# Token order in a one-core encoder step: prefix, prompt, sample; queries without the prefix's rows; value keys in blocks of 128; the third phase's operand sums in one run

## The chip, the core and the metric

The kernel runs on one core of a Trainium2 chip. The core has a matrix engine (TensorE, PE in the profile, with its weight loads in a row of their own, PEld), a vector engine (DVE), a scalar/activation engine (ACT), GpSimd (POOL) and SyncE (SP), which issues nearly all DMAs here. Data lies in on-chip memory of 128 partitions; matmul results go to eight PSUM banks of 128 x 512 fp32. The metric is device time in microseconds for one launch, the median of several runs.

## The reference, cut to what matters

One layer of an encoder on two kinds of rows: a new stream of 512 prompt frames with 16 learned prefix rows ("meta tokens") in front, and 64 sample frames of a running stream that has 128 cached rows.

```python
xp = concat([meta, x_prompt])                 # 16 + 512 rows
h = rmsnorm(x);  z = h @ w_in                 # 2048 -> 1024 q | 1024 k | 1024 v | 512 cq | 256 ckv | 64 kr
# group A, 8 heads: two softmaxes with a shared relative-position bias, p = p0 - lam * p1, o = p @ v, rmsnorm
# group B, 8 heads: q = rmsnorm(cq) @ w_uq, latent keys and values from rmsnorm(ckv) @ w_ukv, one rotary key
# chunk-causal: a frame sees its own chunk of 64 frames, all earlier ones, and the prefix
x = x + concat([o_a, o_b]) @ w_out
h = rmsnorm(x);  x = x + (silu(h @ w_gate) * (h @ w_up)) @ w_down      # 2048 -> 5632 -> 2048
y_prompt = rmsnorm(xp)[16:];  y_sample = rmsnorm(xs)                  # the prefix's own output isn't returned
# also returned: keys, values, latents and rotary keys of prefix + prompt, and of the sample
```

So the prefix's rows are needed as keys and values only, never as queries.

## The kernel before, in words

All 592 rows (T) are columns: activations lie transposed, 128 features by rows. Matrix products are made of three matmuls in a reduced-precision fp32 format, each operand split in a high and a low part: ACT copies the high part (`split`, a copy on ACT), DVE subtracts it from the source for the low part. With two column halves, one 128 x 128 weight block costs six matmuls. The order of columns is sample (64), prefix (16), prompt (512); `OWN` = 80 is sample and prefix together, `TQ` = 576 the rows that are asked as queries, `QH` = 288 its half, `TH` = 296 the half of T.

Phase 1 reads the rows (`load_x`), transposes them on TensorE (`transpose_x`, six pieces of the token list `tok`), sums squares for the norm on ACT (`squares`), and then runs the 31 column blocks of `w_in` as projections of 16 x 6 matmuls (`project`). Group A's heads run between them: scores (`scores`), softmax, and `probabilities_times_values`, which transposes the probabilities on TensorE into one PSUM bank ("tp"), has ACT and DVE evict and split them, and multiplies. Its keys go in pieces: the 80 own columns, then four blocks of 128 prompt keys, then the sample's cached and own keys.

Phase 2 does group B the same way, with the output projection's first half (`mix_out`) as filling between the heads. In phases 1 and 2 the order of TensorE's instructions is written out: `Streams` runs generators against a planned clock (each matmul advances it, each bank is taken and given back at planned times), and TensorE keeps that program order. Other engines' instructions are ordered by a planner from their readiness, each engine then runs its own queue strictly in order.

Phase 3 is the output projection's second half: for each of 16 rows of blocks two halves of 24 matmuls, with weights fetched and split two halves ahead (`fetch`), the residual added, the row scaled (`xg`), its square accumulated on POOL (`sq2`, `rb2`), and for every second row the seven operands of a Strassen-Winograd product (`token_operands`), four of them sums made on POOL. Phase 4 is the feed-forward with those operands (`winograd`), then the final norm, transposes and output DMAs (`finish`), which go through the token halves of 288 in groups of 96 rows.

In `token_operands` POOL's sums share a tile, one overwriting the other after its operand was split:

```python
t = sum_tile()
pin(G.tensor_tensor(t, b12, b11, op=ALU.subtract))
operand(m, 5, t)
yield
pin(G.tensor_tensor(t, b22, t, op=ALU.subtract))
operand(m, 6, t)
```

and the phase's loop runs the whole generator at once:

```python
if i % 2:
    for _ in token_operands(ma, i // 2, xe, xg):
        pass
```

Of the kernel before, what the change touches and what calls it, by code (L numbers as in the profile page):

```python
# [19 lines left out]
P = 128  # L20
# [4 lines left out]
T = OWN + SEQ  # L25
TH = T // 2
TP = T + PAST
TQ = NS + SEQ
QH = TQ // 2
KEPT = ((0, NS, 0), (OWN, SEQ, NS))  # L30
# [101 lines left out]
def encoder_step(  # L132
# [78 lines left out]
    def project(ps, wsrc, xs, dup=False):  # L211
        for hf in range(2):
            wh, wl = weights(
                wsrc[hf * 8 * P:(hf + 1) * 8 * P, :].rearrange("(k p) c -> p k c", p=P), 8, P, dup)
            for k in range(8):
                kc = hf * 8 + k
                mm3([ps[:, 0, 0:TH], ps[:, 1, 0:TH]], wh[:, k, :], wl[:, k, :],
                    halves(xs[kc][0]), halves(xs[kc][1]), kc == 0, kc == KC - 1)
                yield 0

    def probabilities_times_values(pt_b, p5, vkeys, vpast, pool, tbank, pso, pace, done):
# [6 lines left out]
        def times_values(n, p, c0):  # L228
            (vh, vl), (ph, pl) = vkeys[n], p
            for m, (a, b) in enumerate(((vh, ph), (vh, pl), (vl, ph))):  # L230
                PE.matmul(po[:, c0:512], a, b, start=(n == 0 and m == 0), stop=(n == 4 and m == 2))
# [3 lines left out]
        yield from st.take("tp")  # L235
        tp = tbank()
        for b in range(4):
            PE.transpose(tp[0:OWN, b * P:(b + 1) * P], pt_b[b][:, 0:OWN], ident)
        hi, lo = evac("po", tp, OWN, 512)
        last = [(0, (hi[0:OWN], lo[0:OWN]), 0)]  # L240
        st.give("tp", 1.9)
        for t in range(2):
            yield pace
            yield from st.take("tp")
            w = 512 - P * t
            tp = tbank()
            for b in range(t, 4):
                PE.transpose(tp[:, (b - t) * P:(b - t + 1) * P], pt_b[b][:, OWN + t * P:OWN + (t + 1) * P], ident)
            hi, lo = evac(f"pk{t}", tp, P, w)
            for a in last:  # L250
                times_values(*a)
            last = [(1 + t, (hi, lo), t * P)]
            st.give("tp", 1.9)
        yield pace
        yield from st.take("tp")
        tp = tbank()
        for n, (t, b) in enumerate(((2, 2), (2, 3), (3, 3))):
            PE.transpose(tp[:, n * P:(n + 1) * P], pt_b[b][:, OWN + t * P:OWN + (t + 1) * P], ident)
        hi, lo = evac("pk2", tp, P, 384)
        for a in last:  # L260
            times_values(*a)
        last = [(3, (hi[:, 0:256], lo[:, 0:256]), 256), (4, (hi[:, 256:384], lo[:, 256:384]), 384)]
        st.give("tp", 1.7)
        yield pace
        yield from st.take("tp")
        tp = tbank()
        PE.transpose(tp[:, 0:NS], p5[:, 0:P], ident[0:NS, 0:NS])
        PE.transpose(tp[0:NS, NS:2 * NS], p5[:, P:P + NS], ident[0:NS, 0:NS])
        p5h = pool.tile([P, 2 * NS], F32R, name="p5h")
        p5l = pool.tile([P, 2 * NS], F32R, name="p5l")  # L270
        for rows, c in ((P, slice(0, NS)), (NS, slice(NS, 2 * NS))):
            split(p5h[0:rows, c], p5l[0:rows, c], tp[0:rows, c])
        for a in last:
            times_values(*a)
        done(po, NS, TQ)
        st.give("tp", 1.7)
# [5 lines left out]
        own = [v[0:NS] for v in vkeys[0]]  # L282
        for (vh, vl), ph, pl in ((vpast, p5h[:, 0:NS], p5l[:, 0:NS]),
                                 (own, p5h[0:NS, NS:2 * NS], p5l[0:NS, NS:2 * NS])):
# [3 lines left out]
        done(po5[:, 0:NS], 0, NS)  # L288
        st.give("po", 1.0)

    def scores(b, sp, passes):

        if b == 4:
            n, W, q0 = NS, P + NS, 0
            pieces = [(0, 0, P, T), (0, P, NS, 0)]
            flat = True
        else:
            n, W, q0 = P, 144 + P * b, OWN + P * b
            flat = W <= 512
            pieces = [(0, 0, W, NS)] if flat else [(0, 0, W // 2, NS), (1, 0, W // 2, NS + W // 2)]  # L300
        for bank, o, w, k0 in pieces:
            for i, (q, k) in enumerate(passes):
                PE.matmul(sp[0:n, bank, o:o + w], q[:, q0:q0 + n], k[:, k0:k0 + w],
# [11 lines left out]
    def sum_squares(pq, tiles, tile_of):  # L315
        for n, z in enumerate(tiles):
            sq = tile_of("sq")
            S.activation(sq, z, AF.Square)
            yield 1.2
            for i in range(2):  # L320
                PE.matmul(pq[:, i, 0:TH], ones, sq[:, i * TH:(i + 1) * TH],
# [19 lines left out]
    with ExitStack() as ph:  # L341
# [21 lines left out]
        xs1 = list(zip(xh, xl))  # L363
        rb = az.tile([P, T], F32, name="rb")
# [5 lines left out]
        tok = [(0, OWN), (OWN, P), (208, 88), (TH, P), (424, P), (552, 40)]  # L370
# [4 lines left out]
        with tc.tile_pool(name="xn", bufs=1) as xn, tc.tile_pool(name="xc", bufs=1, side="right") as xc:  # L375
# [11 lines left out]
            ssp = az.tile([P, 6, 4], F32, name="ssp")  # L387
# [4 lines left out]
            def load_x(cg):  # L392
                cs = slice(cg * 512, (cg + 1) * 512)
                for j, (o, n) in enumerate(tok):
                    t = xn.tile([P, 512], F32, name="xn", tag=f"xn{j}", bufs=4)
                    if j == 0:
                        load(t[0:NS, :], x_sample[:, cs])
                        load(t[NS:OWN, :], meta[:, cs])
                    else:
                        load(t[0:n, :], x_prompt[o - OWN:o - OWN + n, cs])  # L400
                    xt_in[cg, j] = t

            def transpose_x(kc):
                cg, k = kc // 4, kc % 4
                if kc % 2 == 0:
                    sp = sbig("pxt")
                    banks = [sp[:, 0, 0:TH], sp[:, 1, 0:TH]]
                else:
                    banks = [tbank("pxa")[:, 0:TH], pso.tile([P, 512], F32, name="pxb", tag="po")[:, 0:TH]]
                for j, (o, n) in enumerate(tok):  # L410
                    b = o // TH
                    PE.transpose(banks[b][:, o - b * TH:o - b * TH + n],
                                 xt_in[cg, j][0:n, k * P:(k + 1) * P], ident[0:n, 0:n])
                xt = xn.tile([P, T], F32, name="xt", tag="xt", bufs=7)
                g = gA[:, kc:kc + 1]
                if kc % 2 == 0:
                    split_scaled(hv(xh[kc]), hv(xl[kc]), ev(sp), g)
# [1274 lines left out]
```

## Time and profile before

| | |
|---|---|
| median of 3 runs | 2481.91 us (2481.8 to 2481.93) |
| the profiled execution: its time, its span | 2478.58 us, 2476.8 us |
| granted TensorE clock, mean | 0.994 |
| busy share of the span: PE, PEld, DVE, ACT, POOL | 97%, 95%, 72%, 47%, 30% |
| start up to the first full stretch of matmuls | 0 to about 25 us |
| phase 1 | to about 550 us |
| phase 2 | to 842.7 us |
| phase 3 | 842.7 to 960.1 us |
| phase 4 and output | 960.1 to 2476.8 us |

Busy time counts a matmul from its start to a modelled end, so neighbouring matmuls overlap; what one costs in a stream is the distance from start to start. In the timeline a line stands for a run of like instructions: start, busy time, engine, line, operation, output<-input, shape, count, and in brackets how long the engine sat idle before it and who released it. In the rows by line and form the idle time before a group stands behind the bar, with its releasers. In the waits: who waited for whom, total microseconds, times, the longest. Line 125 and lines 108 and 112 are helpers through which ACT, DVE and SP, and TensorE's ordered matmuls and transposes, are issued, so tiles tell more than lines there.

### The profile page before, as it was taken

How to read it: one execution, taken by the hardware profiler on the slowest of the kernel's cores; microseconds unless marked ns; L12 is line 12 of the kernel's file. 1: busy time of each engine (PE TensorE's matmuls, PEld its weight loads, DVE VectorE, ACT ScalarE, POOL GpSimd, SP SyncE). 2: the span in 40 equal slices, each digit the busy share in tenths (PEclk: the TensorE clock that was granted, in tenths of full speed). 3: DMA queues.
4: the chain of work that ended last, by engine and by line, in shares of the span. 5: the costliest groups of instructions: out<-in, count | busy, mean ns of one | idle time of the engine just before them, and what ended most of it. 6: DMA issues, size and time to landing. Idle time of an engine off the chain costs nothing.

```text
span 2476.8 us, 44895 instructions
## 1 busy us (share of the span) xinstructions
PE 2409.9 (97%) x17697; PEld 2364.3 (95%) x17697; DVE 1781.8 (72%) x2831; ACT 1159.4 (47%) x2212; POOL 733.8 (30%) x590
## 2 busy tenths in 40 slices
PE   8999999999999999999999999999999999999998
PEld 6999999988999888999999999999999999999998
DVE  5555555556556567778878888788787988888874
ACT  5444444334444444445555455555554433333345
POOL 0000000000000165554555545545444322222223
PEclk9999999999999999999999999999999999999999
DMA  7533222334232454324444344334443965645332
GB/s 218 146 93 85 82 81 79 89 92 149 85 100 80 148 157 134 120 96 144 155 136 142 129 146 160 128 133 147 141 158 127 310 218 191 228 154 176 105 111 86
DMA packets 336485, 338.05 MB, mean 136 GB/s; under 512 B 25827, under 2 KB 279658, under 8 KB 336274
## 3 DMA queue, kind: packets, MB, share of 16 engines
q1 hardware_dynamic: 335714, 333.12, 42.1%
q8 instruction: 139, 2.28, 0.4%
q0 software_dynamic: 560, 2.06, 0.2%
q14 instruction: 72, 0.59, 0.1%
HBM read 265.21 MB, written 72.61 MB: 136 GB/s over the span
## 4 chain that ended last, share of the span: by engine, by line
PE 58%; DVE 1%; POOL 1%; DMA 1%; ACT 0%; issue 0%; DVEq 0%; POOLq 0%; SPq 0%
PE m L1155 38%; PE m L1159 19%; PE m L205 1%; DMA raw<-in_ffn_w_down 1%; DVE b L125 0%; PE m L1522 0%; DVE wl L125 0%; ACT b L125 0%; POOL b L1509 0%; POOL ws L1124 0%; POOL c L1327 0%; PE m L1536 0%; POOL b L1504 0%; ACT y L125 0%; DVE y L125 0%
## 5 line engine op out<-in xcount | busy, mean ns | idle before, releaser
L1155 PE MATMUL m<-b,wh 128*128 128x288 f32 x7168 | 1048.6, 295 | 4.9 <-ACT wh L125 2.6
L1155 PEld LDWEIGHTS m<-b,wh 128*128 128x128 f32 x7168 | 984.4, 189 | 7.3 <-ACT wh L125 4.9
L1159 PE MATMUL m<-b,wl 128*128 128x288 f32 x3584 | 579.3, 297 | 2.2 <-DVE wl L125 2.2
L1124 POOL TENSOR_TENSOR ws<-raw 128x512 f32<-128x512 f32 (+1 forms) x258 | 367.4, 1432 | 546.0 <-DVE wl L125 289.0
L1159 PEld LDWEIGHTS m<-b,wl 128*128 128x128 f32 x3584 | 513.6, 188 | 3.2 <-DVE wl L125 3.2
L125 ACT ACTIVATE wh<-ws 128x512 fp32r<-128x512 f32 (+1 forms) x340 | 283.5, 846 | 394.8 <-PE m L1155 250.4
L125 DVE TENSOR_TENSOR wl<-ws,wh 128x512 fp32r<-128x512 f32 (+1 forms) x340 | 388.8, 1154 | 93.8 <-ACT wh L125 93.5
L125 DVE TENSOR_TENSOR wl<-raw,wh 128x512 fp32r<-128x512 f32 x387 | 359.0, 953 | 7.5 <-ACT wh L125 6.6
L125 ACT ACTIVATE wh<-raw 128x512 fp32r<-128x512 f32 x387 | 227.4, 620 | 286.9 <-PE m L1155 264.6
L108 PE MATMUL ps<-xh,wh 128*128 128x296 f32 x960 | 221.8, 313 | 3.5 <-ACT wh L125 3.5
L108 PE MATMUL ps<-xh,wl 128*128 128x296 f32 x960 | 211.4, 302 | 0.9 <-DVE wl L125 0.7
L108 PE MATMUL ps<-xl,wh 128*128 128x296 f32 x960 | 211.3, 302 | 0.0
L125 DVE TENSOR_TENSOR y<-y,m 128x288 f32<-128x288 f32 x312 | 140.2, 451 | 89.1 <-PE m L1159 69.5
L108 PEld LDWEIGHTS ps<-xh,wh 128*128 128x128 f32 x960 | 157.8, 192 | 7.9 <-ACT wh L125 4.2
L108 PEld LDWEIGHTS ps<-xh,wl 128*128 128x128 f32 x960 | 157.7, 191 | 1.8 <-DVE wl L125 1.8
L108 PEld LDWEIGHTS ps<-xl,wh 128*128 128x128 f32 x960 | 158.2, 191 | 0.0
L125 DVE TENSOR_TENSOR ws<-ws,raw 128x512 f32<-128x512 f32 (+1 forms) x129 | 112.1, 872 | 63.7 <-POOL ws L1124 61.4
L125 DVE TENSOR_TENSOR wl<-wr,wh 128x1024 fp32r<-128x1024 f32 (+1 forms) x110 | 119.2, 1084 | 34.9 <-ACT wh L125 33.3
L125 ACT ACTIVATE wh<-wr 128x1024 fp32r<-128x1024 f32 (+1 forms) x110 | 101.7, 929 | 55.8 <-PE ps L108 47.5
L1327 POOL TENSOR_TENSOR c<-c,rb 128x576 f32<-128x576 f32 x44 | 70.9, 1612 | 168.6 <-ACT c L125 168.6
L598 POOL MEMSET bias<- 64x64 f32 x8 | 1.2, 144 | 382.8 <-DMA bias<-tsk 274.1
L1435 POOL TENSOR_TENSOR c<-c 128x576 f32<-128x576 f32 x42 | 73.8, 1757 | 85.1 <-DVE c L125 81.3
(342 smaller groups left out, 3161.7 us busy)
## 6 DMA issues: line engine op xcount, KB each, us to landing
raw<-in_ffn_w_gate SPq DMA_DIRECT2D x44, 1024.0 KB, 6.7
raw<-in_ffn_w_up SPq DMA_DIRECT2D x44, 1024.0 KB, 6.9
raw<-in_ffn_w_down SPq DMA_DIRECT2D x39, 1024.0 KB, 6.0
partspill<-parts SPq DMA_DIRECT2D x126, 288.0 KB, 2.1
b<-partspill SPq DMA_DIRECT2D x126, 288.0 KB, 6.0
wr<-in_w_in SPq DMA_DIRECT2D x60, 512.0 KB, 4.0
wr<-in_w_out SPq DMA_DIRECT2D x16, 512.0 KB, 4.1
wr<-in_w_out SPq DMA_DIRECT2D x32, 256.0 KB, 3.8
```

What stands on the lines that cost most here:

```text
L108: self.tc.keep_in_program_order(self.pe.matmul(out, lhsT, rhs, start=start, stop=stop))
L125: ins = issue(*args, **kwargs)
L205: PE.matmul(outs[i], w, x[i], start=start and p == 0, stop=stop and p == 2)
L598: G.memset(bias[0:64, 464:528], -BIG)
L1124: engine.tensor_tensor(w[:, k:k + m, :], pick(xs), pick(ys), op=op)
L1155: PE.matmul(banks[p], wh[:, k, :], x, start=first and new and k == 0 and x is hi, stop=False, skip_group_check=not new)
L1159: PE.matmul(banks[p], wl[:, k, :], hi, start=False, stop=last and k == n - 1, skip_group_check=not new)
L1327: G.tensor_tensor(g[:, f, :], g[:, f, :], rb2, op=ALU.mult)
L1435: G.tensor_tensor(w[:, f, :], w[:, f, :], g[:, f, :], op=ALU.mult)
```

## The change

Rows are ordered prefix (16), prompt (512), sample (64). Queries, query latents and everything made of them are taken from column 16 on and have 576 columns, not 592. Prefix and prompt lie together, so keys and values go in four blocks of 128 and a last one of 80 (the prompt's last 16 and the sample's 64); the sample's own and cached keys lie side by side and are scored in one piece of 192. `probabilities_times_values` evicts in four groups, the sample's transposes in the last. The probability tiles of phase 2 are made and their unused ends zeroed once. In phase 3 the squares move from POOL to ACT, the four sums are issued together into tiles of their own (some in rooms of later operands, `last_rooms`), and the seven operand splits are drawn from the generator two after each half-row of matmuls. In `finish` the sample's rows are in the last group of the second half.

```diff
-        tok = [(0, OWN), (OWN, P), (208, 88), (TH, P), (424, P), (552, 40)]
+        tok = [(P * j, P) for j in range(4)] + [(SEQ, OWN)]
...
+        xsq = [(a[:, NM:T], b[:, NM:T]) for a, b in xs1]
...
-                    yield from project(ps, w_in[:, h * P:(h + 1) * P], xs1)
+                    yield from project(ps, w_in[:, h * P:(h + 1) * P], xsq)
...
-                for o, n, c in KEPT:
-                    store(xspill[kc, :, c:c + n], xt[:, o:o + n])
+                store(xspill[kc], xt[:, NM:T])
...
+        last = []
+        for g, blocks in enumerate((((0, 0), (0, 1), (0, 2), (0, 3)), ((1, 0), (1, 1), (1, 2), (1, 3)),
+                                    ((2, 1), (2, 2), (2, 3), (4, 3)), ((3, 2), (3, 3)))):
+            if g:
+                yield pace
             yield from st.take("tp")
             tp = tbank()
+            for n, (t, b) in enumerate(blocks):
+                PE.transpose(tp[:, n * P:(n + 1) * P], pt_b[b][:, t * P:(t + 1) * P], ident)
+            w = len(blocks) * P
+            if g == 3:
+                PE.transpose(tp[:, w:w + NS], p5[:, OWN:OWN + P], ident[0:NS, 0:NS])
+                PE.transpose(tp[0:OWN, w + NS:w + 2 * NS], p5[:, 0:OWN], ident[0:NS, 0:NS])
+                w += NS
+            pair = evac(f"pk{g}", tp, P, w)
...
         if b == 4:
-            n, W, q0 = NS, P + NS, 0
-            pieces = [(0, 0, P, T), (0, P, NS, 0)]
-            flat = True
+            n, W, q0, k0 = NS, P + NS, SEQ, T - NS
...
-            load(bias5, skewed(h, 399, NS, P + NS))
+            load(bias5[:, 0:NS], skewed(h, 527, NS, NS))
+            load(bias5[:, NS:NS + P], skewed(h, 399, NS, P))
...
+            for i in range(2):
+                pb = [aq[0].tile([P, P * (b + 2)], F32, name=f"p{b}{i}") for b in range(4)]
+                for b in range(4):
+                    G.memset(pb[b][:, NM + P * (b + 1):P * (b + 2)], 0.0)
...
-    def token_operands(pool, m, b1, b2):
+    def token_operands(m, b1, b2, t5, t6, t4, t7):
         b11, b12, b21, b22 = quarters(b1, b2)
+        G.tensor_tensor(t5, b12, b11, op=ALU.subtract)
+        G.tensor_tensor(t6, b22, t5, op=ALU.subtract)
+        G.tensor_tensor(t4, b21, t6, op=ALU.subtract)
+        G.tensor_tensor(t7, b22, b12, op=ALU.subtract)
         yield
+        for p, src in ((1, b11), (2, b21), (3, b22), (5, t5), (6, t6), (4, t4), (7, t7)):
+            operand(m, p, src)
+            yield
...
             fetch(2 * i + hf + 2)
+            for _ in range(2):
+                next(making, None)
...
         S.activation(xg, x, AF.Copy, scale=gF[:, i:i + 1])
-        if i == 0:
-            G.tensor_tensor(sq2, x, x, op=ALU.mult)
-        else:
-            G.tensor_tensor(rb2, x, x, op=ALU.mult)
+        if i % 2:
+            if m < 7:
+                sums = [last_rooms[p][:, m % 2, :] for p in (5, 6, 4, 3)]
+            else:
+                sums = [ma.tile([P, QH], F32, name="bs", tag="bs", bufs=4) for _ in range(4)]
+            making = token_operands(m, xe, xg, *sums)
+            next(making)
+        S.activation(sq2 if i == 0 else rb2, x, AF.Square)
+        if i:
             G.tensor_tensor(sq2, sq2, rb2, op=ALU.add)
...
-            s = max(0, NS - o)
-            if s:
-                store(y_sample[o:o + s, cs], ot[0:s])
-            store(y_prompt[o + s - NS:o + n - NS, cs], ot[s:n])
+            r = min(n, SEQ - o)
+            store(y_prompt[o:o + r, cs], ot[0:r])
+            if r < n:
+                store(y_sample[o + r - SEQ:o + n - SEQ, cs], ot[r:n])
```

More of the change, by code (lines that the diff above doesn't have):

```diff
@@ L250, in probabilities_times_values @@
+            pair = evac(f"pk{g}", tp, P, w)
+            if g == 3:
+                own = [pool.tile([P, NS], F32R, name="p5" + x) for x in "hl"]
+                split(own[0][0:OWN], own[1][0:OWN], tp[0:OWN, w:w + NS])
             for a in last:
                 times_values(*a)
-            last = [(1 + t, (hi, lo), t * P)]
+            if g < 2:
+                last = [(g, pair, 0)]
+            elif g == 2:
+                last = [(2, cut(pair, P, 0, 384), P), (4, cut(pair, NM, 384, 512), 384)]
+            else:
+                last = [(3, cut(pair, P, 0, 256), 256)]
@@ L265, in probabilities_times_values @@
[L265 to L274, printed above, removed]
@@ L1174, in encoder_step, with last_room @@
     ws = {}
+    def last_room(p):
+        return bc.tile([P, 2, QH], F32, name=f"b{p}_7")
+    last_rooms = {p: last_room(p) for p in ORDER[:6]}
+    making = iter(())
     def fetch(n):
```

267 lines of the change are left out of this document (117 added, 150 removed).

## The prediction

> **What bounds the kernel now.** I read the page first. Its engine row says who is busy; the windows by stage say where that engine is not, and only there can a reordering gain anything.
>
> ```profile
> PE 2409.9 (97%) x17697; PEld 2364.3 (95%) x17697; DVE 1781.8 (72%) x2831; ACT 1159.4 (47%) x2212; POOL 733.8 (30%) x590
> ```
>
> The stages below were cut at the first and last instruction of each part. Columns: stretch, length, then busy time and count of PE, weight loads, DVE, ACT, POOL, granted clock, DMA share, GB/s.
>
> ```profile
> 60.00:550.00 490.00, 477.25 (x3441) 466.05 (x3439) 280.85 (x603) 220.20 (x452) 3.90 (x16) 0.99 0.33 91
> ...
> 575.00:831.80 256.80, 248.84 (x1816) 238.60 (x1816) 146.86 (x290) 102.63 (x230) 11.32 (x36) 0.99 0.29 88
> 831.80:842.70 10.90, 6.41 (x39) 4.47 (x36) 6.37 (x12) 5.90 (x13) 0.00 (x0) 1.00 0.63 200
> 842.70:960.10 117.40, 110.38 (x768) 104.51 (x768) 75.74 (x120) 53.52 (x103) 70.19 (x59) 0.99 0.55 166
> ...
> 1012.00:2466.40 1454.40, 1450.87 (x10908) 1448.16 (x10907) 1169.84 (x1658) 698.76 (x1268) 618.76 (x451) 1.00 0.46 152
> ```
>
> The feed-forward part (1012 to 2466) is TensorE alone: 1450.87 us over 10908 matmuls, 133.0 ns from start to start, nearly all with 288 columns. The change leaves it alone, so 1454 of the 2477 us stay. The first phase (60 to 550) and the second (575 to 832) are TensorE too, at 97%: there a saved column counts at full price. The third phase (842.7 to 960.1) is different. Its 768 matmuls of 288 columns would take 768 x 133.0 ns = 102.1 us and it lasts 117.4: 15.3 us are lost there.
>
> **The change, part by part.**
>
> *Queries without the prefix's rows.* 296 columns become 288. Of the 31 projections of the first phase (the row counts 960 of one pass; with the two other passes and the 96 under another name that makes 31 x 96) the 8 query and the 4 query-latent ones shrink: 12 x 96 = 1152 matmuls. In the second phase 12 query projections of 24 shrink: 288.
>
> ```profile
> L108 PE MATMUL ps<-xh,wh 128*128 128x296 f32 x960 | 221.8, 313 | 3.5 <-ACT wh L125 3.5
> ```
> ```profile
> 544.90 0.43 PE L108 MATMUL ps<-xh,wh 128*128 128x296 f32 x2
> ...
> 549.54 0.43 PE L108 MATMUL ps<-xh,wl 128*128 128x296 f32 x2
> ```
>
> Between these two lines of the timeline lie 34 matmuls of 296 columns in 4.64 us: 136.5 ns each, against 133.0 for 288. So 1440 x 3.5 ns = **-5.0 us**, all on the bounding engine. The narrower evictions on DVE and ACT lie beside matmuls and I cost them at nothing.
>
> Here a page speaks against the change. The Trainium skill, "TensorE: Matmul & The Clock Gate", section "Back-to-back issue gap", gives a sustained spacing of 81 ns at 128 columns and 131 ns at 512; an estimate from that slope makes eight columns worth 1.0 ns, hence -1.5 us in place of -5.0. The rows above do not agree with it: they stand at 133.0 and 136.5 ns well below 512 columns, and I keep their difference.
>
> *The sample's keys in one piece.* A latent head's sample scores took ten matmuls (128 and 64 columns) and now take five of 192; a differential head's eight become four.
>
> ```profile
> 827.18 0.22 PE L108 MATMUL sp<-kmh,qnh 128*64 128x128 f32 x1
> ...
> 827.74 0.51 PE L108 MATMUL ps<-mxh,wh 128*128 128x288 f32 x2
> ```
>
> Ten such matmuls took 0.56 us, 56 ns each at either width. No row shows 192 columns under 64 weights: it costs between 56 ns (width free) and 133 ns (the 288-column one). Down the slope above (3.5 ns for 8 columns) from 133 it would be 91 ns; I take that, since it lies between and both ends are measured. Latent: 8 x (0.56 - 5 x 0.091) = 0.8; differential: 8 x (8 x 0.056 - 4 x 0.091) = 0.7: **-1.5 us**, ends -4.0 and +1.5. The differential bias for the samples comes in two loads, one more a head on SP: hidden, as the load stands a head ahead; uncovered it would cost one issue, some 0.5 us a head.
>
> *Start.* The tokens come in five pieces, not six, so 16 transposes and 4 row squares on ACT go.
>
> ```profile
> 42.73 0.83 PE L112 MATMUL pxt<-ident,xn 80*128 80x80 f32 x6
> 43.49 0.54 PE L108 MATMUL ps<-xh,wh 128*128 128x296 f32 x2
> ```
> ```profile
> 13.45 0.63 ACT L125 ACTIVATE junk<-xn 40x512 f32<-40x512 f32 x1
> 13.99 0.19 ACT L125 ACTIVATION_READ_ACCUMULATOR junk<-xn 40x1 f32 x1
> 14.08 0.73 ACT L125 ACTIVATE xh<-pxt,gT 128x592 fp32r<-128x592 f32 x1
> ```
>
> Six transposes occupy 0.76 us, 0.127 each: at most 16 x 0.127 = 2.0; if the price goes by columns (592 stay) it is nothing. I take **-1.5**, nearer the per-instruction end because pieces of 40 to 128 columns share that time. The square of the 40-row piece stands straight ahead of the first eviction that the first projection needs: 0.63 + 0.19, **-0.8 us**. The stores of the residual input halve in number (16 fewer SP issues): hidden either way, nothing.
>
> *Values by 128 keys.* Before, a head multiplied 512 (80 keys), 512, 384, 256 and 128 columns three times; after, 512, 512, 384, 128 and 256. Same sum, and 16 transposes before and after. What changes is the rounds through the one transpose bank: five become four. Where other work fills the gaps that is worth nothing on TensorE. The last head has no cover:
>
> ```profile
> 837.58 0.55 PE L112 MATMUL tp<-ident,p 128*128 128x128 f32 x3 [0.47 <-DVE pk1l L125]
> ...
> 839.30 0.33 PE L112 MATMUL tp<-ident,p 64*128 64x64 f32 x2 [0.64 <-DVE pk2l L125]
> ```
>
> A round there takes 1.72 us. It goes, but the third one now moves 512 columns rather than 384, and the last product must wait for its own eviction, which the sample's small round used to cover: I give back half, **-0.9 us**, ends -1.7 and +1.0. For the other 15 heads: nothing, ends -2 and +3. The zeroing of the probability tiles moves out of the heads to one place on POOL; the rotary product of POOL is queued behind it, but POOL is busy for 11 of 257 us there. Uncovered, it would delay one product by a few microseconds once.
>
> *Third phase.* The waits of the weight loads in its window, and what the other engines did:
>
> ```profile
> PEld m L205 <- ACT wh L125: 5.9, 12, 0.8
> PEld m L205 <- DVE wl L125: 5.5, 14, 0.7
> ```
> ```profile
> L1201 POOL TENSOR_TENSOR sq<-sq,rb 128x576 f32<-128x576 f32 x14 | 21.4, 1531 | 1.1
> L1200 POOL TENSOR_TENSOR rb<-x 128x576 f32<-128x576 f32 x14 | 20.8, 1485 | 29.7 <-issue 15.5 <-DVE x L125 14.2
> L125 ACT ACTIVATE wh<-wr 128x512 fp32r<-128x512 f32 x30 | 18.1, 617 | 6.5 <-PE m L205 3.2 <-DMA wr<-in_w_out 2.6 <-DVE wl L125 0.7
> ...
> L125 ACT ACTIVATE b<-bs 128x288 fp32r<-128x288 f32 x29 | 12.9, 445 | 42.0 <-POOL bs L1060 21.0 <-POOL bs L1063 16.5 <-POOL bs L1072 2.5
> L125 ACT ACTIVATE xg<-x,gT 128x576 f32<-128x576 f32 x15 | 11.7, 778 | 12.0 <-DVE x L125 11.9
> ```
>
> This is where the change has most to win. TensorE waits 11.4 us for weight splits. ACT itself sits idle 42.0 us in front of the copies of POOL's sums, because POOL first squares (1.49 us) and accumulates (1.53 us), and each sum overwrites the tile that ACT and DVE must have read. Weight splits queued behind such a copy come late. After: four sums in four tiles, straight from the scaled rows, ahead of POOL's accumulation; the square on ACT; the seven operand splits handed out two per half-row of matmuls. ACT gains 16 squares, at the 0.78 us of the scaling of the same shape 12.5 us: 66 of 117. POOL loses 16 x 1.49 = 24 us. No engine comes near the 102 us of matmuls. What is late next is the weights' own DMA, already 2.6 us of ACT's wait, and the start of the stage. I leave about 2 us of the 11.4: **-9.5 us**, ends -11.4 and +1 (16 squares in front of splits, 12.5 us, eating the gain).
>
> *Into the feed-forward.* The last operands stand between the first weight splits:
>
> ```profile
> 965.45 0.44 ACT L125 ACTIVATE b<-bs 128x288 fp32r<-128x288 f32 x1 [3.02 <-POOL bs L1063]
> ...
> 967.43 1.32 PE L1155 MATMUL m<-b,wh 128*128 128x288 f32 x8 [1.82 <-ACT wh L125]
> ```
>
> ACT waits 3.02 us for POOL, TensorE then 1.82 for ACT. With the sums first on POOL (three microseconds of square and accumulation gone from ahead of them) that wait goes: **-1.8 us**, ends -2.6 and 0.
>
> *The end.* The samples' rows now come last: four more output DMAs fall behind the last matmul.
>
> ```profile
> 2466.42 6.74 SPq L125 DMA_DIRECT2D out<-b  x12
> ```
> ```profile
> 2468.00:2474.00 6.00, 0.40 (x4) 0.14 (x2) 1.69 (x3) 1.26 (x3) 0.00 (x0) 0.86 0.98 306
> ```
>
> Twelve issues take 6.74 us, 0.56 each, so four more cost up to 2.2 us. But the DMA engines are 98% busy there and the bytes stay: then nothing. Nearer that row, **+0.5 us**.
>
> Sum: -5.0 -1.5 -1.5 -0.8 -0.9 -9.5 -1.8 +0.5 = -20.5 us. The profiled execution lasted 2478.58 us (span 2476.8 and 1.8 around it), so 2458.1 for it; the median of the runs, 2481.91, stands 3.3 us higher: 2461.4.
>
> **The rivals.**
> 1. *The third phase doesn't speed up*, because ACT's squares, or the weights' DMA, take the place of POOL's sums in front of the splits. For it: ACT runs in order and the 2.6 us are there already. Against: ACT has half the stage free. Then -11.0, 2470.9.
> 2. *The first two phases fall in another order.* TensorE runs a written-out order whose spacing is planned; each shorter matmul shifts it. The profile has this in one row:
>
> ```profile
> PE sp L108 <- DVE nm L125: 9.1, 9, 1.7
> ...
> PE tp L112 <- DVE pk0l L125: 3.8, 3, 2.8
> PE tp L112 <- DVE pol L125: 3.7, 4, 1.4
> ```
>
> Nine waits of the sample's scores. All gone: 2452.3; doubled: 2470.5.
> 3. *Slower: the eviction rounds lose their cover.* With four rounds in place of five, each head might run them back to back, as the last does; an uncovered round costs about 0.8 us of its 1.72 (the rest is its matmuls). 15 heads x 3 rounds x 0.8 = 36 us: 2481.9 - 20.5 + 36 = 2497. It decides from 26 of the 45 rounds. Against: before, 7 waits were left uncovered over all heads, and the planned spacing of the bank is unchanged.
> 4. *Columns are nearly free*, worth 1.0 ns for eight: 1440 x 1.0 = 1.5, so 2464.9. Against: the two spacings measured. By the Trainium skill's section above.
> 5. *It adds up to nothing*: the waits only move, 2481.9 within 0.2% (5 us, about what a measurement of this kernel can tell from no change). Against: the columns alone give more.
>
> **How the numbers follow.** Forecast as summed 0.66 (its own range 2455 to 2467); rival 1 0.14; rival 2 0.12, half each way; rival 4 0.04; rival 3 0.03; rival 5 0.01. The time is the first. The range 2450 to 2474 takes in rivals 1, 2 and 4 and the summed bounds of the scores and rounds (+3 each); it leaves out 3 and 5. Faster 0.95, within 0.2% 0.02, slower 0.03.
>
> **What would show it.** Right: 296-column rows fall to 19 x 96 matmuls and 288-column ones appear in the first phase at 133 ns; the third phase lasts near 108 us and the weight loads' waits for splits fall under 3 us; ACT no longer idles before the sums' copies; the first weight split of the feed-forward doesn't wait on POOL; sixteen output issues at the end, taking about 7 us. Wrong: a third phase still near 117 us with ACT's squares ahead of the splits, or the score bank's waits far from 9 us.

## The result, and the profile after

The changed kernel takes 2451.93 us (median of 4 runs, 2450.92 to 2452.85) against 2481.92 us for the kernel before in runs beside it: ratio 0.9878, 95% interval 0.9862 to 0.9893. That is 30.0 us, where the prediction had 20.5 and a range that ended at 2450. The profiled execution took 2450.92 us (span 2449.1), 1.0 us below its median; the one of before stood 3.3 us below its own, so 2.3 of the 30.0 us are only this difference, and the two traces have 27.7 us to explain.

The engine row of the page after, then the windows by stage (columns as in the prediction). Each stage is cut where the first matmul of the next one begins.

```profile
PE 2391.8 (98%) x17607; PEld 2350.9 (96%) x17607; DVE 1778.9 (73%) x2815; ACT 1161.0 (47%) x2204; POOL 714.6 (29%) x553
```
```profile
0.00:55.00 55.00, 43.80 (x277) 38.25 (x278) 32.71 (x59) 32.33 (x70) 0.20 (x4) 1.00 0.83 245
```
```profile
55.00:534.40 479.40, 471.12 (x3412) 459.10 (x3410) 277.80 (x594) 218.54 (x444) 4.07 (x17) 0.99 0.34 92
534.40:546.80 12.40, 1.94 (x6) 0.82 (x4) 8.14 (x12) 7.06 (x11) 5.32 (x8) 0.63 0.81 251
546.80:812.10 265.30, 260.12 (x1846) 246.88 (x1847) 156.85 (x304) 109.93 (x238) 7.84 (x14) 0.99 0.32 96
812.10:823.30 11.20, 7.31 (x39) 5.21 (x37) 6.75 (x11) 6.03 (x12) 0.00 (x0) 0.89 0.70 222
823.30:931.20 107.90, 106.42 (x768) 104.54 (x768) 81.77 (x119) 60.34 (x118) 47.38 (x44) 0.98 0.59 178
931.20:960.60 29.40, 27.55 (x193) 27.11 (x194) 24.46 (x39) 14.01 (x27) 11.59 (x9) 0.94 0.47 154
960.60:2374.30 1413.70, 1408.64 (x10565) 1405.24 (x10565) 1156.33 (x1614) 672.51 (x1208) 609.71 (x422) 1.00 0.46 154
```

The kernel before, cut at the same places, gives the first column of this table (us). The third is what the prediction's terms come to when they are sorted by stage.

| stage | before | after | moved | predicted |
|---|---|---|---|---|
| start | 59.4 | 55.0 | -4.4 | -2.6 |
| first phase | 490.4 | 479.4 | -11.0 | -4.4 |
| handover between the phases | 8.6 | 12.4 | +3.8 | 0 |
| second phase | 273.4 | 265.3 | -8.1 | -1.8 |
| its last head, alone | 10.9 | 11.2 | +0.3 | -0.9 |
| third phase | 117.4 | 107.9 | -9.5 | -9.5 |
| into the feed-forward | 29.0 | 29.4 | +0.4 | -1.8 |
| feed-forward | 1413.1 | 1413.7 | +0.6 | 0 |
| end | 74.6 | 74.8 | +0.2 | +0.5 |

Three things need a reason: the first phase won over twice its forecast, the second phase won what the handover lost and more, and the stretch into the feed-forward won nothing.

### The profile page after: what moved, and what is told of

The parts are those of the page before. It is cut to its first block, busy times and chain, and to the rows that moved or that the text cites. A ratio compares the mean times of both kernels' runs of the same rounds, so it can differ in the third digit from the quotient of the medians.

```text
span 2449.1 us, 44580 instructions
## 1 busy us (share of the span) xinstructions
PE 2391.8 (98%) x17607; PEld 2350.9 (96%) x17607; DVE 1778.9 (73%) x2815; ACT 1161.0 (47%) x2204; POOL 714.6 (29%) x553
## 4 chain that ended last, share of the span: by engine, by line
PE 52%; DVE 1%; DMA 0%; issue 0%; POOL 0%; ACT 0%; DVEq 0%; POOLq 0%; SPq 0%
PE m L1138 33%; PE m L1142 17%; PE m L204 2%; DVE wl L124 0%; PE m L1521 0%; DMA raw<-in_ffn_w_down 0%; DVE b L124 0%; DMA b<-sumspill 0%; POOL ws L1107 0%; DVE ws L124 0%; PE m L1535 0%; DVE y L124 0%; ACT wh L124 0%; POOL b L1508 0%; DVE c L124 0%
## 5 line engine op out<-in xcount | busy, mean ns | idle before, releaser
L1107 POOL TENSOR_TENSOR ws<-raw 128x512 f32<-128x512 f32 (+1 forms) x258 | 373.4, 1457 | 543.4 <-DVE wl L124 263.0
L107 PE MATMUL ps<-xh,wh 128*128 128x296 f32 (+1 forms) x960 | 218.8, 309 | 1.4 <-ACT wh L124 1.4
L107 PE MATMUL ps<-xl,wh 128*128 128x296 f32 (+1 forms) x960 | 210.3, 300 | 1.5 <-DVE xl L124 1.5
L107 PE MATMUL ps<-xh,wl 128*128 128x296 f32 (+1 forms) x960 | 209.3, 299 | 0.7 <-DVE wl L124 0.6
L124 ACT ACTIVATE parts<-c 128x1 fp32r<-128x1 f32 x252 | 81.2, 322 | 37.5 <-DVE c L124 31.8
```

The lines of the kernel that those rows point to most:

```text
L107: self.tc.keep_in_program_order(self.pe.matmul(out, lhsT, rhs, start=start, stop=stop))
L124: ins = issue(*args, **kwargs)
L1107: engine.tensor_tensor(w[:, k:k + m, :], pick(xs), pick(ys), op=op)
```

## The experiments

The kernels below ran on three occasions, each time beside the kernel before, which took 2481.81, 2480.00 and 2480.74 us by its medians. The changed kernel's 2451.93 is from the first result (2481.92 beside it). So a difference against 2451.93 carries up to 2 us of that, and one of less than 2 us says nothing; ratios are against the kernel before beside each.

**One half of the change at a time.** `p3_only` is the kernel before with the new `token_operands` and third-phase loop alone; `p3_undone` is the changed kernel with the old ones. The cut shows a few lines of the edit; the tiles for the sums and the two draws per half-row belong to it.

```diff
 # p3_only, on the kernel before; p3_undone takes the same lines out again
+        if i % 2:
+            ...
+            making = token_operands(m, xe, xg, *sums)
+            next(making)
+        S.activation(sq2 if i == 0 else rb2, x, AF.Square)
```

> The kernel before with the third phase's part of the change alone (whole rows to ACT's squares, sums in one run, operand splits drawn two by two). If the parts of the change do not touch each other, its third phase lasts 107.9 us as in the changed kernel against 117.4, all stages ahead of it stay as before (490.5 and 273.4 us for the two attention phases), the stretch into the feed-forward stays at 29.0 to 29.4, and the time is 2472.0 to 2472.8 us, ratio 0.9960 to 0.9965. Rival: the third phase gets faster only because less is left over from the second phase; then it stays above 112 us and the time above 2476.

> The changed kernel with the third phase put back as it was before. If the parts add up: third phase 117.4 us, first phase 479.4 and second 265.6 as in the changed kernel, time 2461.0 to 2461.8 us (9.1 to 9.9 above the changed kernel), and all that is left of the gain, 20 us against the kernel before, lies in the start and the two attention phases, where the prediction had 13. Rival: a part of the 11.1 and 7.8 us won in the attention phases came from a planned order that the third phase's edit moved; then these two stages differ from 479.4 and 265.6 by over 1 us.

`p3_only` took 2473.07 us against 2481.81 for the kernel before, ratio 0.9963 (0.9950 to 0.9975). `p3_undone` took 2462.52, ratio 0.9928 (0.9913 to 0.9942), 10.6 above the changed kernel. The third phase of each in the windows, `p3_only` first:

```profile
845.00:952.00 107.00, 105.21 (x768) 103.76 (x769) 82.53 (x121) 60.55 (x118) 47.41 (x44) 0.99 0.61 183
```
```profile
824.50:943.10 118.60, 111.51 (x769) 105.39 (x769) 76.09 (x119) 53.43 (x103) 70.21 (x59) 0.98 0.54 162
```

The third phase follows its own edit (107.0 and 118.6) and nothing else does: `p3_undone`'s two attention phases last 479.7 and 266.0 us. The halves add up to 28.0 of the 30.0 us, 8.7 and 19.3.

**What in the third phase does it.** `squares_pool` puts the square back on POOL; `operands_at_once` draws all seven splits straight after the sums.

```diff
 # squares_pool
-        S.activation(sq2 if i == 0 else rb2, x, AF.Square)
+        G.tensor_tensor(sq2 if i == 0 else rb2, x, x, op=ALU.mult)
 # operands_at_once
-            next(making)
+            for _ in making:
+                pass
```

> The changed kernel with the sixteen squares of the third phase back on POOL, behind the four sums; all else of the third phase as changed. Theory: what the phase won came from the sums standing ahead of POOL's other work and from the splits drawn two by two; then the square's place matters little, the phase lasts 108 to 110 us and the time is 2452 to 2454. Rival: it came from POOL being relieved of 24 us; then ACT waits for the sums again, the weight loads' waits for splits return to 5 to 11 us, and the phase lasts 112 to 117: 2456 to 2461.

> The changed kernel with the seven operand splits of the third phase drawn all at once behind the sums, and not two per half-row of matmuls. Theory: splits of weights queue behind copies that wait for POOL's sums, so drawing them apart is what keeps TensorE fed; then the weight loads' waits rise from under 1 us to 4 to 8 and the phase lasts 111 to 115: 2455 to 2459. Rival: the sums' early place is enough, 107.9 to 109: 2452 to 2453.

`squares_pool` took 2462.01 us, ratio 0.9922 (0.9906 to 0.9939); `operands_at_once` 2456.00, ratio 0.9896 (0.9881 to 0.9911). The third phase's window and the weight loads' largest waits in it (total us, times, longest), of `squares_pool`, then of `operands_at_once`, then the waits of the changed kernel:

```profile
823.60:940.70 117.10, 111.39 (x768) 105.34 (x768) 74.51 (x118) 53.40 (x103) 71.43 (x59) 0.98 0.54 165
...
PEld m L204 <- ACT wh L124: 6.5, 13, 0.9
PEld m L204 <- DVE wl L124: 3.3, 13, 0.3
```
```profile
821.40:936.70 115.30, 107.93 (x768) 105.61 (x768) 82.63 (x121) 60.94 (x118) 47.24 (x44) 0.97 0.55 169
...
PEld m L204 <- DVE wl L124: 6.3, 7, 1.2
PEld m L204 <- ACT mh L124: 1.9, 1, 1.9
```
```profile
PEld m L204 <- DVE ml L124: 0.9, 2, 0.5
PEld m L204 <- DVE wl L124: 0.5, 1, 0.5
```

With the square on POOL the whole gain of the phase is gone, against my theory. POOL's timeline shows why: first `squares_pool`, then the changed kernel, the same pair of half-rows.

```profile
855.14 1.47 POOL L1199 TENSOR_TENSOR rb<-x 128x576 f32<-128x576 f32 x1 [2.58 <-issue]
856.70 1.52 POOL L1201 TENSOR_TENSOR sq<-sq,rb 128x576 f32<-128x576 f32 x1
858.18 1.03 POOL L1051 TENSOR_TENSOR b<-xg,b 128x288 f32<-128x288 f32 x1
```
```profile
854.22 0.81 POOL L1051 TENSOR_TENSOR b<-xg,b 128x288 f32<-128x288 f32 x1 [3.31 <-ACT xg L124]
854.98 0.81 POOL L1053 TENSOR_TENSOR b<-xg 128x288 f32<-128x288 f32 x1
855.74 1.03 POOL L1052 TENSOR_TENSOR b<-xg,b 128x288 f32<-128x288 f32 x1
856.73 1.64 POOL L1201 TENSOR_TENSOR sq<-sq,rb 128x576 f32<-128x576 f32 x1
```

In the program the three sums stand ahead of the square. On POOL's queue they don't: the square needs only the row that DVE has made, and it and the accumulation (L1201) come out ahead of the sums that need ACT's scaled row. So `squares_pool` lost the early sums too, and it can't tell POOL's load from its order. It does show that in these two kernels the sums come early only when the square is off POOL. A kernel with the square on POOL but queued behind the sums was not run. In it ACT waited for the sums about as it did before the change (35.6 us in two groups, 42.0 then; in the changed kernel its largest wait for one of them is 4.3 us in all):

```profile
ACT b L124 <- POOL b L1051: 18.1, 7, 2.6
ACT b L124 <- POOL b L1050: 17.5, 7, 2.7
```

Drawing the splits apart is worth 4.1 us in the runs: without it, each of seven pairs of half-rows ends in a wait for DVE's weight split, 6.3 us in all. (Its window shows more, 7.4 us: 1.7 is one late tile of rows at the start of the phase, and some 1.3 is time at a lower granted clock, 0.97 in place of 0.98.) Both edits are needed for the whole gain.

**The rounds of the transpose bank.** The prediction gave the fifth round's going 0.9 us. `five_rounds` puts it back into the changed kernel; `rounds_only` takes it out of the kernel before and changes nothing else; `planned_wide` changes only PE's order.

```diff
 # five_rounds
-                                    ((2, 1), (2, 2), (2, 3), (4, 3)), ((3, 2), (3, 3)))):
+                                    ((2, 1), (2, 2), (2, 3), (4, 3)), ((3, 2), (3, 3)), ())):
 # rounds_only, behind the three transposes of the fourth round
+        PE.transpose(tp[:, 384:384 + NS], p5[:, 0:P], ident[0:NS, 0:NS])
+        PE.transpose(tp[0:NS, 448:448 + NS], p5[:, P:P + NS], ident[0:NS, 0:NS])
         hi, lo = evac("pk2", tp, P, 384)
 # planned_wide, in the planner's cost of a matmul
+        n = TH if n == QH and rhs.dtype == F32R else n
```

> The changed kernel with the sample's transposed probabilities evicted in a fifth round of their own, as before; same columns, same keys in one piece, same third phase. Theory of the rounds: the single transpose bank costs a wait at every round, and one round fewer is what the prediction left out; then phase one comes back by 5 to 7 us (484 to 487), phase two by 5 to 6.5 (270.5 to 272), the waits ahead of transposes rise from 0.1 to about 2 us in phase one and from 1.2 to about 5 in phase two, and the time is 2462 to 2465 us. Rival, the planned order: the 12.7 us beyond the prediction came from a luckier order that any edit of the streams would lose or keep; then the time changes by some other amount, with no return of waits at the transposes. Rival, nothing in it: within 2 us of 2451.9.

> The kernel before with one part of the change alone: the sample's two transposes go into the fourth round's bank and its own fifth round is dropped; columns, key pieces, token order and third phase stay as before. The fifth round put back into the changed kernel cost 15.1 us, where the prediction had 0.9. Theory of the rounds: a round costs whatever the rest of the kernel looks like; then the kernel before gains 8 to 15 us from this alone, 2467 to 2474, in the two attention phases. Prediction's view: nothing outside the last head, 2480 to 2482. Third theory: the fifth round was dear in the changed kernel only since it drove the last head's scores out of the second phase (25.5 us for the last head in place of 11.2), and its price elsewhere is what the first phase showed, 4 to 5 us; then 2475 to 2479.

> The changed kernel with the same instructions, but with the planner told that the 288-column products of the projections last as long as 296-column ones, so that only the order on PE moves. Theory of the rounds: the order is worth little, 2451 to 2454 us, each attention phase within 1.5 us of 479.4 and 265.6. Rival, the planned order: the gain beyond the prediction is an accident of the order, and another order loses 4 to 13 us of it: 2456 to 2465.

`five_rounds` took 2467.04 us, ratio 0.9947 (0.9932 to 0.9961), 15.1 above the changed kernel. `rounds_only` took 2476.26 against 2480.00, ratio 0.9980 (0.9971 to 0.9989). `planned_wide` took 2450.32, ratio 0.9876 (0.9861 to 0.9891). The windows of `five_rounds` (first phase, second, last head), and the first phase of `rounds_only`:

```profile
55.80:542.60 486.80, 475.47 (x3412) 462.72 (x3410) 278.26 (x601) 218.75 (x452) 4.08 (x17) 0.99 0.33 91
555.20:816.80 261.60, 255.06 (x1809) 243.16 (x1809) 153.07 (x294) 105.07 (x232) 8.40 (x14) 0.99 0.31 96
816.80:842.30 25.50, 18.42 (x75) 13.98 (x74) 12.41 (x29) 10.65 (x29) 0.00 (x0) 0.60 0.54 177
```
```profile
58.40:544.20 485.80, 475.45 (x3445) 464.84 (x3444) 280.87 (x603) 221.79 (x453) 3.90 (x16) 1.00 0.33 92
```

The profiled execution of `five_rounds` lay 4.9 us above its median, so its windows show more than the 15.1 us. They are two things. The larger one is in the last head: 25.5 us in place of 11.2. There the fifth round has pushed that head's scores out of the second phase, and they stand alone on TensorE at a clock of 0.60; the second phase is 3.7 shorter for it. The other is 7.4 us in the first phase. Some 3.0 of these are pairs of like matmuls that start over 25 ns late without any recorded wait, 57 in place of 29. Most of them are not scattered: they stand in rows of 13, each matmul about 110 ns late, in stretches of 3.4 us in which the granted clock is one half. `five_rounds` has four such stretches in its first phase, the changed kernel two. This is one of them, and as long a window behind it (TensorE alone: length, busy time and count, granted clock, DMA share, GB/s):

```profile
231.40:234.80 3.40, 3.40 (x17) 0.51 0.69 203
235.00:238.40 3.40, 3.40 (x28) 1.00 0.09 14
```

They come and go from one execution to another: `p3_only`, whose first phase is that of the kernel before, has 53 late pairs and four stretches where before has 30 and two. About 4.4 us are left for eight heads. `rounds_only` has -4.6 there, one stretch in place of two and 1.7 of it in such pairs, so -2.9. A round fewer in the first phase is worth 3 to 4.4 us. That is the third theory's view; the runs of `rounds_only` say 3.7 in all, 2.7 to 7.2 by their interval.

It isn't a wait at the transpose bank, as my theory had it. Half of it or more, 2.2 to 2.5 us, is the wait of the sample's scores for DVE; the rest has no row. TensorE's largest wait in the first phase: before (already shown) 9.1 us in 9, then `five_rounds`, `rounds_only` and the changed kernel:

```profile
PE sp L107 <- DVE nm L124: 9.1, 9, 1.1
```
```profile
PE sp L108 <- DVE nm L125: 6.6, 7, 1.0
```
```profile
PE sp L107 <- DVE nm L124: 6.9, 7, 1.1
```

Nine waits go with five rounds and seven with four, in every trace: nine in before, `p3_only` and `five_rounds`, seven in all others. How a round makes them is not shown. One of the two more in `five_rounds`, and what DVE did ahead of it:

```profile
229.63 0.30 PE L107 MATMUL sp<-kh,q00s 128*64 128x192 f32 x1 [1.00 <-DVE nm L124]
```
```profile
228.20 0.76 DVE L124 SCALAR_TENSOR_TENSOR z<-ps,rb 128x576 f32<-128x576 f32 x1 [1.67 <-PE ps L107]
```

DVE had been idle, and then scaled a finished projection (`z`) before it came to the scores. There is no eviction of probabilities ahead of it. So the fifth round seems to move the scores to where a projection ends, which is argued and not shown. The half-clock stretches follow these waits: each one in a first phase begins within 3 us of a pair of them, about 1.0 us each, or, once (`p3_only`), just behind the weight split's wait at 76 us.

Another order on PE (`planned_wide`) moved nothing that the runs can tell, but it was a small one: 399 of 17607 matmuls stand at another place.

**The price of columns and of key pieces.** `wide_queries` computes the twelve query projections of the first phase for 296 columns, planned as 288; `two_pieces` scores the sample's keys in two pieces.

```diff
 # wide_queries (the eviction drops the first eight columns)
-                    yield from project(ps, w_in[:, h * P:(h + 1) * P], xsq)
+                    yield from project(ps, w_in[:, h * P:(h + 1) * P], xs1, planned=QH)
 # two_pieces
+        if b == 4:
+            pieces = [(0, 0, NS, k0), (0, NS, P, T)]
```

> The changed kernel with the first phase's twelve query projections computed for all 296 columns again (the extra eight are thrown away by the eviction), planned as 288 so that the order on PE stays. 1152 matmuls are wider by 8 columns. Prediction's price, 3.5 ns each: +4.0 us, 2456.0, and start-to-start times of 136.5 ns in place of 133.0. Rival, 1.0 ns for eight columns: +1.2 us, 2453.1. Third: the columns are free behind the score waits, 2452.

> The changed kernel with the sample's keys scored in two pieces again (64 and 128 columns, 72 more matmuls). Prediction: +1.5 us, 2453.4. By the start-to-start time of the score matmuls in the two traces (1.28 us won in the first phase and 1.15 in the second): +2.4, 2454.3. Rival: the pieces change the planned order as well and the time moves by over 4 us.

`wide_queries` took 2457.62 us (2453.28 to 2460.12), ratio 0.9904 (0.9889 to 0.9919): +5.7, or +7.6 when each is taken from the kernel before beside it. The same last projection of the first phase on TensorE's timeline, in the changed kernel and then in `wide_queries`:

```profile
530.19 0.42 PE L107 MATMUL ps<-xh,wl 128*128 128x288 f32 x2
...
534.13 0.42 PE L107 MATMUL ps<-xh,wl 128*128 128x288 f32 x2
```
```profile
538.22 0.43 PE L107 MATMUL ps<-xh,wl 128*128 128x296 f32 x2
...
542.32 0.43 PE L107 MATMUL ps<-xh,wl 128*128 128x296 f32 x2
```

Thirty matmuls lie between each two lines: 131.3 and 136.7 ns. Over all evenly spaced ones of the first phase it is 132.2 (964 of them) and 136.5 (2401): 4.3 ns for eight columns, not 3.5. Times 1152 that is 5.0 us. The columns are not nearly free. (Its first phase has three half-clock stretches where the changed kernel has two; that may be the rest.)

`two_pieces` took 2450.91 us (2448.56 to 2454.27), ratio 0.9884 (0.9867 to 0.9900): 1.0 us below the changed kernel, but 0.9 above it when each is taken from the kernel before beside it. So the runs can't tell the 1.5 to 2.4 that were expected from nothing. The score matmuls of the two phases do take longer in its trace, 33.3 and 31.3 us from start to start against 32.6 and 30.1, together 1.9. Its profiled execution took 2448.56 us all the same: it has one half-clock stretch fewer in the first phase, and its unchanged feed-forward happened to last 2.7 us less (1411.0).

**The handover.** After the change TensorE waits 8.1 us here for a table. SP's queue in the changed kernel, and TensorE's first matmul behind it:

```profile
535.45 0.42 SPq L124 DMA_DIRECT2D mspill<-o  x1
...
539.25 0.34 SPq L729 DMA_DIRECT2D mxl<-mspill  x1
...
541.06 0.43 SPq L124 DMA_DIRECT2D kmsk<-c_kmask  x1
```
```profile
546.84 0.45 PE L111 MATMUL pkr<-ident,rn 128*128 128x128 f32 x1 [8.09 <-DMA kmsk<-c_kmask]
...
547.99 0.68 PE L107 MATMUL ps<-mxl,wh 128*128 128x288 f32 x2
...
549.91 0.68 PE L107 MATMUL ps<-mxh,wl 128*128 128x288 f32 x2
```

```diff
 # handover
-            (G if h < H - 1 else nc.sync).dma_start(f32(mixl[h]), mspill[h])
...
         load(qmsk, c_qmask)
+        load(f32(mixl[H - 1]), mspill[H - 1])
```

> The changed kernel with one load moved on SP's queue: the last head's mixed rows, which must wait for their own store to land, are loaded after the four small tables of the second phase (compressed keys, rotary keys, two masks) and not ahead of them. Theory: the 12.4 us between the phases hold 8.1 us of waiting for a table that stood behind that load on SP; moved, the stretch falls to 8 to 9 us and the time to 2448 to 2449. Rival: the first product then waits for the mixed rows themselves, or for the store, and the stretch stays at 11 to 12.4: 2451 to 2452.

It took 2451.03 us, ratio 0.9880 (0.9865 to 0.9894). The stretch fell to 8.0 us as expected, and the time hardly moved: the second phase rose from 265.3 to 268.3. TensorE's timeline in `handover`:

```profile
542.49 0.45 PE L111 MATMUL pkr<-ident,rn 128*128 128x128 f32 x1 [4.13 <-DVE cql L124]
...
544.13 0.85 PE L107 MATMUL ps<-mxh,wh 128*128 128x288 f32 x2 [0.76 <-ACT mxh L124]
546.25 0.85 PE L107 MATMUL ps<-mxl,wh 128*128 128x288 f32 x2 [1.27 <-DVE mxl L124]
```

Behind the table's wait three others come up, for DVE's split of the latents and for the two splits of the mixed rows, now loaded last: 6.2 us of the 8.1 come back as these. Handover, second phase and last head together last 288.9 us in the changed kernel and 287.4 in `handover`; the 0.9 us of the medians are less than the runs can tell.

**Into the feed-forward, and both edits together.** `last_stepped` draws the last pair's operands inside the feed-forward's first products; `both_better` does this and moves the load as well.

```diff
 # last_stepped
-    for _ in making:
-        pass
...
-    winograd(fw, ma, [raw0], range(4), None, banks0, stag=("wr", WR_BUFS))
+    winograd(fw, ma, [raw0], range(4), None, banks0, step=lambda: next(making, None), stag=("wr", WR_BUFS))
+    for _ in making:
+        pass
```

> The changed kernel with the last operands (the pair m=7) drawn step by step inside the feed-forward's first products, and not all ahead of its first weight splits. The prediction had the 1.8 us wait of TensorE at the first weight split of the feed-forward gone; it stayed. Theory: it stayed since ACT still copies the last four sums, waiting for POOL, ahead of the third weight split; drawn later, the stretch into the feed-forward falls from 29.3 to 27.5 and the time to 2450. Rival: the products soon need the last operands themselves and wait for those: 29 to 31 us, 2452 to 2454.

> The changed kernel with two edits: the last operands drawn inside the feed-forward's first products, and the mixed rows' load behind the second phase's small tables. The load's move alone gave 4.4 us at the handover and took 3.1 back in the second phase, 0.9 us faster in the runs. Theory: the two add up, 2448.5 to 2450 us, with the two stages at 8 and 27.5. Rival: neither is worth anything outside its own stage, 2451 to 2452.

ACT in the kernel before (start, us, instruction), ACT and TensorE in the changed kernel, and the stretch's windows, `last_stepped` and then `operands_at_once`, which has the changed kernel's order there:

```profile
961.48 0.62 ACT L125 ACTIVATE wh<-raw 128x512 fp32r<-128x512 f32 x1
```
```profile
934.52 0.44 ACT L124 ACTIVATE b<-bs 128x288 fp32r<-128x288 f32 x1 [0.52 <-POOL bs L1052]
935.49 0.44 ACT L124 ACTIVATE b<-bs 128x288 fp32r<-128x288 f32 x1 [0.53 <-POOL bs L1053]
935.84 0.61 ACT L124 ACTIVATE wh<-raw 128x512 fp32r<-128x512 f32 x1
```
```profile
936.50 2.01 PE L1138 MATMUL m<-b,wh 128*128 128x288 f32 x8 [1.81 <-ACT wh L124]
```
```profile
929.50:956.80 27.30, 26.27 (x193) 25.70 (x194) 24.50 (x36) 13.86 (x27) 12.43 (x9) 1.00 0.51 166
```
```profile
936.70:965.10 28.40, 26.07 (x192) 25.61 (x193) 24.01 (x38) 13.86 (x27) 11.62 (x9) 1.00 0.49 159
```

In the kernel before, the third weight split of the feed-forward began at 961.48, 1.4 us after the first product and ahead of the copy that waited 3.02 us for POOL; the 1.82 us there were a wait for the fourth. In the changed kernel it stands behind all seven operand copies, 4.6 us after the first product, and the 1.81 us are a wait for it. So the wait came one split earlier and kept its size. Drawn in steps, the stretch falls from 29.4 to 27.3, in `both_better` as well. About 1.0 us of that is not the wait: the changed kernel's row has a clock of 0.94, a half-clock stretch behind its wait, and with the same wait at full clock the stretch lasts 28.4 in `operands_at_once`. `last_stepped` took 2449.09 us, ratio 0.9874 (0.9859 to 0.9889); `both_better` 2448.42 (2444.74 to 2450.41), ratio 0.9866 (0.9851 to 0.9881), the lowest median here, 3.5 us below the changed kernel, or 2.4 when each is taken from the kernel before beside it. The intervals of these two and of the changed kernel overlap, so no gain of the whole time is shown, only the stage's own 1.1 us at equal clock.

## Why the prediction was right, and where its terms were off

The time lay inside the range, at its fast end, and that it did is in part luck: the third phase came out as worked out, but in the traces 7.2 us more than the sum were won, mostly by terms that the sum had too small or at nothing. The range reached that far for other reasons (rival 2's waits gone, the bounds of the scores and rounds). By its steps:

- **Third phase, -9.5: right in size (9.5), and on the mechanism the runs correct one point.** The wait for splits fell from 11.4 us to under 2. The prediction gave the early sums and the square's move as two things; on POOL's queue, as it came out in these kernels, the second is the condition of the first. Rival 1 (ACT's squares take POOL's place) is out: ACT has 60.3 of 107.9 us of work.
- **Columns, -5.0: a term that was sized too small.** It took 3.5 ns for eight columns from the feed-forward's spacing of 133.0; 288 columns in the attention phases stand at 132.2, so 4.3 ns and 6.2 us for the 1440. `wide_queries` puts the columns back at +5.7 to +7.6 for 1152. Rival 4 had 1.0 ns, the Trainium skill's slope ("TensorE: Matmul & The Clock Gate", "Back-to-back issue gap"). The run speaks against it: by that slope `wide_queries` would have lost 1.2 us.
- **Key pieces, -1.5: 1.9 us in the score matmuls; the whole time can't tell it from nothing.**
- **Start, -2.6 with its columns: too small, 4.4.** No single cause was tried here. The transposes of the start and the gaps behind them went from 18.3 to 13.0 us, start to start, where the term had 16 x 0.127; the projections gave 1.0 of it back.
- **Rounds, -0.9 and nothing for 15 heads: the step that failed.** "Where other work fills the gaps that is worth nothing on TensorE" overlooked the sample's scores, which wait for DVE: nine such waits with five rounds, seven with four. A round in the first phase is worth 3 to 4.4 us, of which 2.2 to 2.5 are these waits. Why the round makes them stays open. Rival 2 named those waits and had them go or double with the order; they went from nine to seven with the round, and stayed at seven in the one small change of order that was run.
- **First phase, 6.6 us more than its terms.** By rows: 2.2 of the score waits; 1.1 of the round of 80 keys (a wait for `pol` that no longer exists); 2.5 of one weight split that TensorE waited for at 76 us and no longer does; 0.9 more for the columns; less 1.3 of two new small waits. Some 1.2 us are left without a row. That the weight split's wait went with the shorter start is argued, not shown: it stays in `rounds_only`.
- **Second phase: what looks like 6 us too much is 1.3.** Handover, second phase and last head belong together: 292.9 us before, 288.9 after, -4.0 against a forecast of -2.7. `handover` shows that a wait moved there comes back elsewhere. The last head alone did not shorten, 10.9 to 11.2, but its row has a clock of 0.89; where no half-clock stretch falls into it (`two_pieces`, `operands_at_once`) it lasts 10.6 to 10.7, so the 0.9 of the forecast was 0.2 to 0.3.
- **Into the feed-forward, -1.8: wrong, +0.4.** ACT's 3.02 us for POOL did fall, to two waits of 0.5, but the third weight split, which stood ahead of the copy of the late sum, now stands behind all seven copies, and TensorE waits as long for it as it had for the fourth. Without the half-clock stretch the stage would be 28.4, 0.6 less than before. `last_stepped` takes the wait out: 27.3.
- **The end, +0.5: 0.2**; sixteen issues took 8.32 us in one row, for 6.74 of twelve.
- **Rival 3 (rounds lose their cover) did not come true**, but `five_rounds` shows something near it: a last head that holds its own scores, with nothing beside them and at a clock of 0.60, lasts 14.3 us longer, of which the second phase wins 3.7 back.

## What to carry to other kernels

A round through a shared bank is not only that bank's time: count the waits of the other streams before and after, also those for an engine that the round doesn't name. Where a window loses a few microseconds and its neighbour wins them, add them up before explaining either. On a queue filled by a scheduler, written order is no order; read from the engine's own timeline that the early work is early. Matmuls that start late without a wait may stand in a half-clock stretch: look at the granted clock of a window as short as that stretch before comparing two stages.

## What the runs showed of the hardware

After the idle 8.1 us at the handover the matmuls of 288 columns ran 240 ns apart (eight in the 1.92 us from 547.99 to 549.91 in the rows above) in place of 132, until about 551: some 2 us beside the wait itself. The Trainium skill, "TensorE: Matmul & The Clock Gate", Part 1 ("The HAM clock gate"), has half the clock after a window of some 3.4 us without work, until another such window has been busy; these rows agree. The stretches of the first phase do not: the one from 231.4 us in `five_rounds` came behind two waits of 1.0 and 1.1 us, with matmuls between them, and lasted 3.4 us all the same. Each costs about 1.4 us (13 matmuls, 110 ns late). Their number isn't fixed by the program: the same first phase had two in before and four in `p3_only`.

The feed-forward is the same program in every run here, and its stretch lasted 1411.0 to 1416.9 us in the profiled executions: a spread of 5.9 us with nothing changed. A stage's own window tells an edit of 2 us that the whole time does not, if the granted clock is the same in both.
